# Split operands of all matmuls at one place modulo 256 bytes, stationary weights 64 bytes behind it

## The chip, the cores and the metric

The kernel runs on one core of one Trainium2 chip. The metric is the device time of one execution in microseconds (us), the median of several runs. A core has TensorE (matmuls), VectorE (DVE), ScalarE (ACT), GpSimd (POOL) and SyncE (SP, which here issues most DMAs), a memory SBUF of 128 partitions for operands and a memory PSUM in which matmuls accumulate.

## The reference

Two blocks over 256 tokens of width 2048, batch 1, all in float32. Cut to what matters:

```python
for i in range(2):                                  # first block
    shift, scale, gate = split((silu(c) @ ada_w[i] + ada_b[i])[:, None, :], 3)
    h = rmsnorm(x, norm_g[i]) * (1.0 + scale) + shift
    y = retention_branch(h, ...) if i == 0 else mla_branch(h, ...)
    x = x + gate * y
x = rmsnorm(x, final_norm_g)
# second block
h = rms_norm(x, attn_norm_gain)                     # then h @ w_in, two kinds of attention,
x = x + mixed(h) @ w_out                            # outputs normed and concatenated
x = x + peer(rms_norm(x, ffn_norm_gain), ...)       # 16384 experts, 8 heads of top 16
out = rms_norm(x, final_norm_gain)
```

retention_branch projects h to q, k, v and g (12,288 columns), mla_branch to two latents, a rope key and g (3,136 columns). peer picks experts by two top-16 lists, and adds, for each token, gate * gelu(expert_down[e] . x) * expert_up[e] over its 128 experts.

## The kernel before

Activations stay in SBUF: x by tokens, and the normed h transposed (hT), so that channels lie on partitions. Weights stream from HBM in pieces of 1 MB: a tile raw of 128 x 2048 float32, which SP loads (line 179, 1184 or 1272), three buffers. Every large product is made of three matmuls on operands split in two: h = the value rounded to float32r, l = the rest. split() (lines 172 and 173) makes them, ACT the rounded half (wh), VectorE the rest (wl), in half tiles of 1,024 columns from a ring of four pairs (halves(), lines 164 to 169), and a fifth pair xh, xl while the experts' second product runs.

Which operand is stationary (loaded as weights of TensorE, 128 columns of it) and which moves differs by place in the program:

- proj_steps (lines 243 to 245): the activations are stationary (hT, zT, zT1, ckvT, cqT, mT, and in the last part of the retention two wide tiles named v and sg), the streamed weights move, mostly 512 columns at once; 424, 416, 384, 272 and 256 in some blocks. For each k of a half tile it does two token blocks of three matmuls.
- turned_steps (lines 271 to 273) for q and k of the retention: the streamed weights are stationary, hT moves, 256 columns.
- hidden() (lines 1214 to 1216), the first product of peer, for all 128 blocks of 128 experts: the expert weights are stationary, hT moves, 256 columns.
- up_steps (lines 1294 to 1296), the second product of peer: the gated hidden values are stationary (Wh, Wl of pool up), the expert weights move (wh, wl or xh, xl), 512 columns.

SBUF is given out in pools, one behind the other: keep, stream (raw, wh, wl), small (tiny tiles), and behind them the pools of a phase (ret, mla, mlah, mix, peer, up and their w). A tile takes its bytes for each partition, rounded up to 32; the first tile of keep lies at byte 16,512, which is 128 modulo 256. Working through the sizes in order gives where operands start modulo 256 bytes. Tiles whose size is no multiple of 256 (colv 928 bytes, cst 4,896, mhalf 32, cact 64, A1 and B1 64 each) stand among the large ones in keep, so that hT starts at 32 and stream at 224. All slices of the operands are multiples of 256 bytes apart, but for the halves of weight pieces with 424, 416 and 272 columns.

| Operand | modulo 256 |
|---|---|
| hT (keep); cqT, ckvT (mla); zT1 (mlah) | 32 |
| raw, wh, wl (stream) | 224 |
| zT and the wide tiles v, sg (ret) | 96 |
| mT (mix) | 64 |
| Wh, Wl, xh, xl (up) | 224 |

The order of work is the program's: background generators (self.bg, tick()) put attention, norms and gates between the steps of projections at fixed rates. ACT's and VectorE's instructions run in the order written, and so do the DMAs that stand in ACT's own queue (nc.scalar.dma_start). cst holds identity, ones, a triangle, an iota, the causal and the dilated masks and small tables, loaded once (line 409). latent() is the second layer, mixed() the attention of the second block; at the start of mixed(), renorm() loads four pieces of a gain on ACT's queue (line 957), which line 967 multiplies in.

Of the kernel before, what the change touches and what calls it, by code (L numbers as in the profile page):

```python
# [10 lines left out]
F32 = mybir.dt.float32  # L11
# [113 lines left out]
class Net:  # L125
    def __init__(self, ctx, tc, a):
        self.ctx, self.tc, self.nc, self.a = ctx, tc, tc.nc, a
        self.keep = ctx.enter_context(tc.tile_pool(name="keep", bufs=1))
        self.st = ctx.enter_context(tc.tile_pool(name="stream", bufs=1))
        self.sm = ctx.enter_context(tc.tile_pool(name="small", bufs=1))  # L130
        self.dr = ctx.enter_context(tc.tile_pool(name="dram", bufs=1, space=bass.MemoryType.DRAM))
        self.ps = ctx.enter_context(tc.tile_pool(name="psum", bufs=1, space=PSUM))
        self.bg = []
        self.nhalf, self.extra = 0, None
        self.places = places()
# [251 lines left out]
    def start(self):  # L387
        nc, keep, a = self.nc, self.keep, self.a
        self.ident = keep.tile([128, 128], F32, name="ident")
        self.colv = keep.tile([128, V_END], F32, name="colv")  # L390
        nc.scalar.dma_start(self.colv, a["vectors"])
        nc.sync.dma_start(self.ident, a["consts"][:, C_ID:C_ID + 128])
        self.cst = keep.tile([128, C_END], F32, name="cst")
        self.xf = [keep.tile([128, D], F32, name=f"x{tb}") for tb in range(2)]
        for tb in range(2):
            nc.scalar.dma_start(self.xf[tb], a["x"][0, tb * 128:tb * 128 + 128, :])
        self.xt = [[self.xf[tb][:, cb * 512:cb * 512 + 512] for cb in range(4)] for tb in range(2)]
        self.mhalf = keep.tile([128, 8], F32, name="mhalf")
        nc.vector.memset(self.mhalf, -0.5)

        self.cact = keep.tile([128, 16], F32, name="cact")
        th = self.tiny(16)
        cc = self.colv[:, V_C:V_C + 16]
        nc.scalar.activation(th, cc, AF.Tanh, scale=0.5)
        nc.vector.scalar_tensor_tensor(th, th, 1.0, cc, op0=OP.add, op1=OP.mult)
        nc.vector.tensor_scalar(self.cact, th, 0.5, None, op0=OP.mult)
        self.ones = self.cst[:, C_ONE:C_ONE + 128]
        self.onesr = keep.tile([128, 128], F32R, name="onesr")
        nc.scalar.dma_start(self.cst, a["consts"])

        nc.vector.tensor_scalar(self.colv[:, V_GN:V_GN + 32], self.colv[:, V_GN:V_GN + 32], 0.5, None, op0=OP.mult)

    def angles(self, pool):
# [5 lines left out]
        self.cos = keep.tile([128, 2, 32], F32, name="cos")  # L419
        self.sin = keep.tile([128, 2, 32], F32, name="sin")  # L420
# [8 lines left out]
        pi = keep.tile([128, 2], I32, name="posi")  # L429
        nc.scalar.dma_start(pi, pos.rearrange("o (b p) -> p (o b)", p=128))  # L430
        pf = keep.tile([128, 2], F32, name="posf")
# [146 lines left out]
    def retention(self):  # L578
# [3 lines left out]
        self.A1 = keep.tile([128, 16], F32, name="A1")  # L582
        self.B1 = keep.tile([128, 16], F32, name="B1")
        with self.phase("ret", 8), self.tc.tile_pool(name="ret", bufs=1) as pool:
            A = pool.tile([128, 16], F32, name="A0")
            B = pool.tile([128, 16], F32, name="B0")
# [195 lines left out]
    def latent(self):  # L782
        nc, a = self.nc, self.a
        w_in, w_out, w_uq, w_ukv = "mla_w_in", "mla_w_out", "mla_w_uq", "mla_w_ukv"
        causal = self.cst[:, C_CAUSAL:C_CAUSAL + 256]
        scale = float(192 ** -0.5)
        with self.phase("mla", 7), ExitStack() as es:
            pool = es.enter_context(self.tc.tile_pool(name="mla", bufs=1))
            G = pool.tile([128, D], F32, name="G1")
            front = ExitStack()  # L790
# [4 lines left out]
            ss = pool.tile([128, 4], F32, name="latss")  # L795
# [16 lines left out]
            def latents():  # L812

                lr = pool.tile([128, 4], F32, name="latr")
# [126 lines left out]
            fa = self.keep.tile([128, 16], F32, name="fa")  # L941
# [6 lines left out]
            self.rtok = self.keep.tile([128, 2], F32, name="rtok")  # L948
# [25 lines left out]
    def mixed(self):  # L974
        nc, a = self.nc, self.a
        w_in, w_out = "w_in_2", "w_out_2"
        causal = self.cst[:, C_CAUSAL:C_CAUSAL + 256]
        with self.phase("mix", 8), self.tc.tile_pool(name="mix", bufs=1) as pool:
            hT, rtok = self.hT, self.rtok
            next(self.norms)  # L980
            norms = self.later(self.norms, 0.9)
            trig = pool.tile([128, 2, 2, 8], F32, name="trig")
            fb = pool.tile([128, 16], F32, name="fb")
            nc.sync.dma_start(fb, bass.AP(tensor=a["forget_bias_2"].tensor, offset=a["forget_bias_2"].offset,
                                          ap=[[0, 128], [1, 16]]))
            lf = pool.tile([128, 2, 16], F32, name="lf")
# [20 lines left out]
            cum = pool.tile([128, 2, 16], F32, name="cum")  # L1007
# [12 lines left out]
            def project(n, g, beside=iter(())):  # L1020
# [17 lines left out]
                for off in (0, 1024):  # L1038
                    def ev(tb, p, off=off):
# [5 lines left out]
                        dst = pool.tile([128, 1, 8, 66], F32, name="qk2", bufs=2)  # L1045
# [26 lines left out]
            def head(n, g, h):  # L1072
# [3 lines left out]
                else:  # L1076
                    mask = lambda tb: self.cst[:, C_DIL:C_DIL + 128] if tb == 0 else \
                        self.cst[:, C_DIL + 128:C_DIL + 384]
# [14 lines left out]
            def finish(n):  # L1093
# [7 lines left out]
                r = pool.tile([128, 2], F32, name=f"r_{n}")  # L1101
# [38 lines left out]
            self.rtok = self.keep.tile([128, 2], F32, name="rtok2")  # L1140
# [3 lines left out]
    def peer(self):  # L1144
# [5 lines left out]
        with self.phase("peer", 4), self.tc.tile_pool(name="peer", bufs=1) as pool:  # L1150
# [30 lines left out]
            def fetch(e):  # L1181
# [4 lines left out]
                for half in range(2):  # L1186
                    dh, dl = self.halves()
# [437 lines left out]
```

## Time and profile before

| | us |
|---|---|
| median of 3 runs | 3252.47 (3251.17 to 3254.47) |
| the profiled execution | 3252.83 |
| its span, first to last instruction | 3251.0 |
| TensorE busy with matmuls | 3159.2 (97%) |
| TensorE weight loads | 2762.0 (85%) |
| VectorE busy | 2366.0 (73%) |
| ScalarE busy | 1558.4 (48%) |
| moved from and to HBM | 216 GB/s over the span |

Matmuls follow each other in a pipeline: each is recorded from its start to its modelled end, and the next begins before that end. So a busy share of 97% doesn't say how fast TensorE works; the time from one start to the next does. Each matmul has its own weight load, which runs beside the matmul before it.

### The profile page before, as it was taken

The page shows a single profiled execution, that of the slowest core. Times are in us where ns is not written, and L with a number is a line of the kernel's source. Part 1 is how long each engine was busy: PE and PEld are TensorE (multiplying, and loading weights), DVE is VectorE, ACT ScalarE, POOL GpSimd, SP SyncE. Part 2 cuts the span into 40 slices and gives each one's busy share as a digit, 9 for nine tenths or more (in the row PEclk, how much of TensorE's full clock was granted, in tenths as well). Part 3 has the DMA queues.
Part 4 walks back from the last instruction along what each step waited for, and adds up shares of the span by engine and source line. Part 5 has one row for each costly group of instructions (what it writes and reads, how often), then busy time and mean ns, then how long its engine had stood idle before and what let it go on. Part 6 is the DMA issues. An engine that isn't in the chain of part 4 may idle for free.

```text
span 3251.0 us, 47605 instructions
## 1 busy us (share of the span) xinstructions
PE 3159.2 (97%) x18562; PEld 2762.0 (85%) x18562; DVE 2366.0 (73%) x3918; ACT 1558.4 (48%) x2162; POOL 414.4 (13%) x487
## 2 busy tenths in 40 slices
PE   4999999999999999999999999999999999999998
PEld 4888977887798888888888999999888898999987
DVE  6898878878787675455669966998766656556665
ACT  3444434344545455555554444555444444444444
POOL 0001210201000320000000312886000000000000
PEclk9999999999999999999999999999999999999999
DMA  8875677786585435444454456777966755555554
GB/s 342 305 268 203 244 270 296 254 300 243 202 289 201 143 130 196 144 153 145 143 185 152 158 198 212 260 242 258 314 238 235 239 201 207 196 202 186 194 194 142
DMA packets 141681, 705.68 MB, mean 217 GB/s; under 512 B 12680, under 2 KB 45832, under 8 KB 67728
## 3 DMA queue, kind: packets, MB, share of 16 engines
q1 hardware_dynamic: 139152, 696.51, 60.9%
q10 hardware_dynamic: 2304, 6.14, 0.5%
q8 instruction: 145, 2.38, 0.3%
q14 instruction: 80, 0.66, 0.1%
HBM read 676.38 MB, written 26.21 MB: 216 GB/s over the span
## 4 chain that ended last, share of the span: by engine, by line
PE 83%; DVE 8%; DMA 4%; issue 3%; ACT 1%; POOL 0%; SPq 0%; DVEq 0%; POOLq 0%; ACTq 0%
PE acc L244 11%; PE acc L245 11%; PE acc L243 11%; PE acc L1294 7%; PE acc L1296 7%; PE acc L1295 7%; PE tmp L1214 5%; PE tmp L1216 5%; PE tmp L1215 5%; DVE wl L173 3%; PE acc L272 2%; PE acc L273 2%; PE acc L271 2%; PE tmp L359 1%; PE acc L1214 1%
## 5 line engine op out<-in xcount | busy, mean ns | idle before, releaser
L173 DVE TENSOR_TENSOR wl<-raw,wh 128x1024 fp32r<-128x1024 f32 (+4 forms) x983 | 1197.2, 1225 | 469.9 <-ACT wh L172 467.6
L172 ACT ACTIVATE wh<-raw 128x1024 fp32r<-128x1024 f32 (+4 forms) x983 | 1018.3, 1044 | 1017.9 <-PE acc L245 343.6
L244 PE MATMUL acc<-wl,hTh 128*128 128x512 f32 (+4 forms) x1280 | 497.4, 389 | 13.1 <-DVE wl L173 13.1
L243 PE MATMUL acc<-wh,hTh 128*128 128x512 f32 (+4 forms) x1280 | 498.3, 391 | 1.5 <-ACT wh L172 1.5
L245 PE MATMUL acc<-wh,hTl 128*128 128x512 f32 (+4 forms) x1280 | 496.7, 388 | 0.0
L1214 PE MATMUL tmp<-hTh,wh 128*128 128x256 f32 x1280 | 361.5, 282 | 0.0
L1216 PE MATMUL tmp<-hTl,wh 128*128 128x256 f32 x1280 | 357.6, 279 | 0.0
L1215 PE MATMUL tmp<-hTh,wl 128*128 128x256 f32 x1280 | 357.5, 279 | 0.0
L1294 PE MATMUL acc<-wh,Wh 128*128 128x512 f32 x812 | 317.4, 391 | 2.8 <-ACT Wh L172 1.5
L1296 PE MATMUL acc<-wh,Wl 128*128 128x512 f32 x812 | 316.5, 390 | 0.9 <-DVE Wl L173 0.9
L1295 PE MATMUL acc<-wl,Wh 128*128 128x512 f32 x812 | 316.3, 390 | 0.0
L244 PEld LDWEIGHTS acc<-wl,hTh 128*128 128x128 f32 x1280 | 241.8, 189 | 63.1 <-DVE wl L173 18.4
L245 PEld LDWEIGHTS acc<-wh,hTl 128*128 128x128 f32 x1280 | 241.8, 189 | 47.9 <-DVE hTl L310 0.4
L243 PEld LDWEIGHTS acc<-wh,hTh 128*128 128x128 f32 x1280 | 241.2, 189 | 46.5 <-ACT wh L172 1.7
L1214 PEld LDWEIGHTS tmp<-hTh,wh 128*128 128x128 f32 x1280 | 240.4, 188 | 0.7
L1216 PEld LDWEIGHTS tmp<-hTl,wh 128*128 128x128 f32 x1280 | 240.9, 188 | 0.1
L1215 PEld LDWEIGHTS tmp<-hTh,wl 128*128 128x128 f32 x1280 | 239.7, 187 | 0.8
L1512 POOL TENSOR_SCALAR oh<-iota,slot 128x128 f16<-128x128 f16 x256 | 208.6, 831 | 168.6 <-DVE iota L1503 87.0
L471 DVE SCALAR_TENSOR_TENSOR w<-raw,cact,w 128x512 f32<-128x512 f32 x240 | 186.9, 779 | 23.1 <-DMA raw<-in_ada_dram 18.5
L1215 PE MATMUL acc<-hTh,wl 128*128 128x256 f32 x640 | 179.9, 281 | 6.9 <-DVE wl L173 6.9
L162 POOL TENSOR_TENSOR tiny<-tiny,mhalf 128x1 f32<-128x1 f32 (+1 forms) x23 | 18.8, 819 | 1303.6 <-DVE tiny L161 1303.6
L1294 PEld LDWEIGHTS acc<-wh,Wh 128*128 128x128 f32 x812 | 152.4, 188 | 36.5 <-DVE x L1303 2.9
(370 smaller groups left out, 5919.8 us busy)
## 6 DMA issues: line engine op xcount, KB each, us to landing
raw<-in_down_dram SPq DMA_DIRECT2D x128, 1024.0 KB, 5.0
raw<-in_up_dram SPq DMA_DIRECT2D x128, 1024.0 KB, 5.0
raw<-in_ret_w_in_dram SPq DMA_DIRECT2D x96, 1024.0 KB, 6.0
raw<-in_ada_dram SPq DMA_DIRECT2D x64, 1024.0 KB, 4.9
raw<-in_w_in_dram SPq DMA_DIRECT2D x44, 1024.0 KB, 4.9
raw<-in_ret_w_out_dram SPq DMA_DIRECT2D x32, 1024.0 KB, 4.9
G<-in_ada_first_dram SPq DMA_DIRECT2D x32, 512.0 KB, 5.8
raw<-in_mla_w_out_dram SPq DMA_DIRECT2D x16, 1024.0 KB, 4.9
```

Of the source, the lines that this page charges most:

```text
L172: self.nc.scalar.activation(h, raw, AF.Copy)
L173: self.nc.vector.tensor_tensor(l, raw, h.bitcast(F32), op=OP.subtract)
L243: nc.tensor.matmul(o, sh, wh[:, j, :], start=(k == 0), stop=False)
L244: nc.tensor.matmul(o, sh, wl[:, j, :], start=False, stop=False)
L245: nc.tensor.matmul(o, sl, wh[:, j, :], start=False, stop=(k == nk - 1))
L1214: nc.tensor.matmul(o, dh[:, s], hh[:, k % 4, :], start=(k == 0), stop=False)
L1215: nc.tensor.matmul(o, dl[:, s], hh[:, k % 4, :], start=False, stop=False)
L1216: nc.tensor.matmul(o, dh[:, s], hl[:, k % 4, :], start=False, stop=(k == 15))
L1294: nc.tensor.matmul(y[tb][c], Wh[:, s], uh[:, u], start=first, stop=False)
L1295: nc.tensor.matmul(y[tb][c], Wh[:, s], ul[:, u], start=False, stop=False)
L1296: nc.tensor.matmul(y[tb][c], Wl[:, s], uh[:, u], start=False, stop=last)
L1512: nc.gpsimd.tensor_scalar(oh2[:, t, :], iota, k2, None, op0=OP.is_equal)
```

## The change

A pool named little is added behind small, with a pad of 56 columns (224 bytes) in front. All tiles whose size is no multiple of 256 bytes move there, out of keep, ret, mla and mix (colv, cst, mhalf, cact, cos, sin, posi, posf, A0, B0, A1, B1, latss, latr, fa, rtok, rtok2, trig, fb, lf, cum, r_f, r_d). cst is cut to its first 456 columns; the causal mask is loaded again in latent(), both masks in mixed(), each with a DMA of its own on ACT's queue into a tile of the phase. qk2 is rounded up to 576 columns. So keep, stream, small and little have sizes that are multiples of 256 bytes, and by the same working all operands of split products start at 128 modulo 256.

The half tiles of halves() grow by 64 columns (256 bytes). Where the weights are stationary (turned_steps through weights(still=True), and fetch() of hidden()), the 1,024 columns used start 16 columns (64 bytes) later in the tile, at 192 modulo 256.

The diff, cut to its core; what is left out moves the other small tiles to self.little in the same way, or takes a mask from the new tiles:

```diff
@@ -31,11 +31,13 @@
 GSCALE = 65536.0
 S1 = 4
 HB = 4
+PAD = 56
+SHIFT = 16
 ADA_RATE = 0.3
 
 
-C_ID, C_ONE, C_TRI, C_IOTA, C_CAUSAL, C_DIL, C_COS2, C_SIN2, C_INVF, C_COLF, C_END = (
-    0, 128, 256, 384, 512, 768, 1152, 1168, 1184, 1216, 1224)
+C_ONE, C_TRI, C_IOTA, C_COS2, C_SIN2, C_INVF, C_COLF, C_CAUSAL, C_DIL, C_ID, C_END = (
+    0, 128, 256, 384, 400, 416, 448, 456, 712, 1096, 1224)
...
@@ -128,6 +130,10 @@
         self.keep = ctx.enter_context(tc.tile_pool(name="keep", bufs=1))
         self.st = ctx.enter_context(tc.tile_pool(name="stream", bufs=1))
         self.sm = ctx.enter_context(tc.tile_pool(name="small", bufs=1))
+
+
+        self.little = ctx.enter_context(tc.tile_pool(name="little", bufs=1))
+        self.little.tile([128, PAD], F32, name="pad")
...
-    def halves(self):
+    def halves(self, still=False):
 
         self.nhalf += 1
         if self.extra is not None and self.nhalf % (HB + 1) == 0:
-            return tuple(self.extra.tile([128, 1024], F32R, name=n, bufs=1) for n in ("xh", "xl"))
-        return tuple(self.st.tile([128, 1024], F32R, name=n, bufs=HB) for n in ("wh", "wl"))
+            t = [self.extra.tile([128, 1088], F32R, name=n, bufs=1) for n in ("xh", "xl")]
+        else:
+            t = [self.st.tile([128, 1088], F32R, name=n, bufs=HB) for n in ("wh", "wl")]
+        o = SHIFT if still else 0
+        return tuple(x[:, o:o + 1024] for x in t)
...
-    def weights(self, name, k, c0):
+    def weights(self, name, k, c0, still=False):
...
-            wh, wl = self.halves()
+            wh, wl = self.halves(still)
...
-            for wh, wl in self.weights(name, k0, c0):
+            for wh, wl in self.weights(name, k0, c0, True):
...
-        self.colv = keep.tile([128, V_END], F32, name="colv")
+        self.colv = self.little.tile([128, V_END], F32, name="colv")
...
-        self.cst = keep.tile([128, C_END], F32, name="cst")
+        self.cst = self.little.tile([128, C_CAUSAL], F32, name="cst")
...
-        nc.scalar.dma_start(self.cst, a["consts"])
+        nc.scalar.dma_start(self.cst, a["consts"][:, :C_CAUSAL])
...
+            causal = pool.tile([128, 256], F32, name="causal")
+            nc.scalar.dma_start(causal, a["consts"][:, C_CAUSAL:C_CAUSAL + 256])
...
+            masks = pool.tile([128, 640], F32, name="masks")
+            nc.scalar.dma_start(masks, a["consts"][:, C_CAUSAL:C_CAUSAL + 640])
+            causal, dil = masks[:, 0:256], masks[:, 256:640]
...
-                        dst = pool.tile([128, 1, 8, 66], F32, name="qk2", bufs=2)
+                        dst = pool.tile([128, 576], F32, name="qk2", bufs=2)[:, :528].rearrange("p (o h d) -> p o h d", o=1, h=8)
...
-                    dh, dl = self.halves()
+                    dh, dl = self.halves(True)
```

## Rows read from the trace of the kernel before

**Rows 1.** The page, parts 1 and 4: busy time, and the chain by engine.
```profile
PE 3159.2 (97%) x18562; PEld 2762.0 (85%) x18562; DVE 2366.0 (73%) x3918; ACT 1558.4 (48%) x2162; POOL 414.4 (13%) x487
...
PE 83%; DVE 8%; DMA 4%; issue 3%; ACT 1%; POOL 0%; SPq 0%; DVEq 0%; POOLq 0%; ACTq 0%
```

**Rows 2.** Stretches: window, length, busy (count) of each engine, clock, DMA share, GB/s.
```profile
660.73:716.26 55.53, 55.53 (x239) 44.80 (x238) 43.49 (x51) 24.70 (x30) 0.00 (x0) 1.00 0.85 306
809.54:840.92 31.38, 31.38 (x136) 25.44 (x135) 20.50 (x26) 15.20 (x23) 0.00 (x0) 1.00 0.56 198
1618.41:1639.02 20.61, 20.61 (x89) 16.59 (x88) 11.75 (x15) 9.40 (x13) 0.00 (x0) 1.00 0.49 173
2291.54:2335.08 43.54, 43.54 (x193) 35.88 (x192) 36.93 (x46) 21.64 (x26) 0.00 (x0) 1.00 1.00 333
```

**Rows 3.** Stretches with 256 moving columns, columns as in rows 2.
```profile
1886.31:1965.81 79.50, 79.50 (x676) 79.50 (x676) 47.28 (x50) 40.11 (x48) 0.00 (x0) 1.00 0.59 206
1854.38:1862.31 7.93, 7.93 (x71) 7.93 (x71) 7.93 (x20) 3.28 (x5) 2.81 (x4) 1.00 0.64 221
1224.89:1232.19 7.30, 7.30 (x64) 7.30 (x63) 5.25 (x12) 6.21 (x16) 0.71 (x1) 1.00 0.79 252
```

**Rows 4.** Groups by form: count | busy us, mean ns of one | idle before.
```profile
L243 PE MATMUL acc<-wh,hTh 128*128 128x512 f32 x1056 | 423.6, 403 | 1.5 <-ACT wh L172 1.5
...
L1214 PE MATMUL tmp<-hTh,wh 128*128 128x256 f32 x1280 | 361.5, 282 | 0.0
...
L1294 PE MATMUL acc<-wh,Wh 128*128 128x512 f32 x812 | 317.4, 391 | 2.8 <-ACT Wh L172 1.5 <-DVE x L1303 1.3
...
L271 PE MATMUL acc<-hTh,wh 128*128 128x256 f32 x512 | 146.8, 288 | 0.1
```

**Rows 5.** Stretches near the start, columns as in rows 2.
```profile
48.00:160.00 112.00, 108.95 (x573) 92.28 (x573) 92.69 (x102) 52.38 (x67) 0.00 (x0) 1.00 0.85 321
160.00:275.00 115.00, 113.55 (x597) 96.08 (x598) 105.82 (x141) 51.66 (x59) 8.88 (x8) 1.00 0.71 251
```

**Rows 6.** Timeline of TensorE, 272 columns: start us, us, engine, line, instruction.
```profile
1240.85 0.29 PE L243 MATMUL acc<-wh,hTh 128*128 128x272 f32 x1
...
1241.62 0.29 PE L243 MATMUL acc<-wh,hTh 128*128 128x272 f32 x1
...
1242.37 0.29 PE L243 MATMUL acc<-wh,hTh 128*128 128x272 f32 x1
...
1243.11 0.29 PE L243 MATMUL acc<-wh,hTh 128*128 128x272 f32 x1
```

**Rows 7.** Timeline of TensorE, 424 columns.
```profile
905.59 0.36 PE L243 MATMUL acc<-wh,hTh 128*128 128x424 f32 x1
...
906.72 0.36 PE L243 MATMUL acc<-wh,hTh 128*128 128x424 f32 x1
...
907.90 0.36 PE L243 MATMUL acc<-wh,hTh 128*128 128x424 f32 x1
```

**Rows 8.** The page, part 5: the two instructions of a split.
```profile
L173 DVE TENSOR_TENSOR wl<-raw,wh 128x1024 fp32r<-128x1024 f32 (+4 forms) x983 | 1197.2, 1225 | 469.9 <-ACT wh L172 467.6
L172 ACT ACTIVATE wh<-raw 128x1024 fp32r<-128x1024 f32 (+4 forms) x983 | 1018.3, 1044 | 1017.9 <-PE acc L245 343.6
```

**Rows 9.** DMA issues: queue, operation, count, KB each.
```profile
cst<-in_consts_dram ACTq DMA_DIRECT2D x1, 612.0 KB
```

**Rows 10.** Timeline of ACT and of VectorE at the start of mixed().
```profile
1224.05 0.36 ACTq L957 DMA_DIRECT2D w<-in_final_norm_g_dram  x1
...
1230.42 2.74 DVE L967 SCALAR_TENSOR_TENSOR x<-x,tiny,w 128x512 f32<-128x512 f32 x4 [0.82 <-POOL tiny L162]
```

**Rows 11.** Timeline of TensorE, f16 matmuls of 128 columns.
```profile
2205.31 1.07 PE L1530 MATMUL acc<-oh,oh 128*128 128x128 f16 x16
2206.18 0.37 PE L1214 MATMUL tmp<-hTh,wh 128*128 128x256 f32 x1
```

More of the change, by code (lines that the diff above doesn't have):

```diff
@@ L397, in start @@
         self.xt = [[self.xf[tb][:, cb * 512:cb * 512 + 512] for cb in range(4)] for tb in range(2)]
-        self.mhalf = keep.tile([128, 8], F32, name="mhalf")
+        self.mhalf = self.little.tile([128, 8], F32, name="mhalf")
         nc.vector.memset(self.mhalf, -0.5)
-        self.cact = keep.tile([128, 16], F32, name="cact")
+        self.cact = self.little.tile([128, 16], F32, name="cact")
         th = self.tiny(16)
@@ L418, in angles @@
         self.sinT = pool.tile([128, 256], F32, name="sinT")
-        self.cos = keep.tile([128, 2, 32], F32, name="cos")
-        self.sin = keep.tile([128, 2, 32], F32, name="sin")
+        self.cos = self.little.tile([128, 2, 32], F32, name="cos")
+        self.sin = self.little.tile([128, 2, 32], F32, name="sin")
         pos = a["positions"]
@@ L428, in angles @@
         nc.vector.tensor_copy(self.onesr, self.ones)
-        pi = keep.tile([128, 2], I32, name="posi")
+        pi = self.little.tile([128, 2], I32, name="posi")
         nc.scalar.dma_start(pi, pos.rearrange("o (b p) -> p (o b)", p=128))
-        pf = keep.tile([128, 2], F32, name="posf")
+        pf = self.little.tile([128, 2], F32, name="posf")
         nc.vector.tensor_copy(pf, pi)
@@ L581, in retention @@
         keep = self.keep
-        self.A1 = keep.tile([128, 16], F32, name="A1")
-        self.B1 = keep.tile([128, 16], F32, name="B1")
+        self.A1 = self.little.tile([128, 16], F32, name="A1")
+        self.B1 = self.little.tile([128, 16], F32, name="B1")
         with self.phase("ret", 8), self.tc.tile_pool(name="ret", bufs=1) as pool:
-            A = pool.tile([128, 16], F32, name="A0")
-            B = pool.tile([128, 16], F32, name="B0")
+            A = self.little.tile([128, 16], F32, name="A0")
+            B = self.little.tile([128, 16], F32, name="B0")
             G = pool.tile([128, D], F32, name="G0")
@@ L784, in latent @@
         w_in, w_out, w_uq, w_ukv = "mla_w_in", "mla_w_out", "mla_w_uq", "mla_w_ukv"
-        causal = self.cst[:, C_CAUSAL:C_CAUSAL + 256]
         scale = float(192 ** -0.5)
@@ L794, in latent @@
             lat = {}
-            ss = pool.tile([128, 4], F32, name="latss")
+            ss = self.little.tile([128, 4], F32, name="latss")
             for n, c0 in (("q", 0), ("kv", 512)):
@@ L812, in latents @@
             def latents():
-                lr = pool.tile([128, 4], F32, name="latr")
+                lr = self.little.tile([128, 4], F32, name="latr")
                 self.rsqrt(lr, ss, 1.0 / 512, 4)
@@ L938, in latent @@
             self.done(beside)
-            fa = self.keep.tile([128, 16], F32, name="fa")
+            fa = self.little.tile([128, 16], F32, name="fa")
             nc.vector.tensor_tensor(fa, self.colv[:, V_FN:V_FN + 16], self.colv[:, V_AT:V_AT + 16], op=OP.mult)
@@ L947, in latent @@
             next(cols)
-            self.rtok = self.keep.tile([128, 2], F32, name="rtok")
+            self.rtok = self.little.tile([128, 2], F32, name="rtok")
             self.norms = self.renorm(ss)
@@ L1006, in ev_forget @@
                 nc.vector.scalar_tensor_tensor(lf[:, tb, :], f, 0.0, ln, op0=OP.min, op1=OP.subtract)
-            cum = pool.tile([128, 2, 16], F32, name="cum")
+            cum = self.little.tile([128, 2, 16], F32, name="cum")
             def forget():
@@ L1076, in head @@
                 else:
-                    mask = lambda tb: self.cst[:, C_DIL:C_DIL + 128] if tb == 0 else \
-                        self.cst[:, C_DIL + 128:C_DIL + 384]
+                    mask = lambda tb: dil[:, 0:128] if tb == 0 else dil[:, 128:384]
                 def done(o, rd):
@@ L1100, in finish @@
                 nc.vector.tensor_reduce(s2, ss.rearrange("p (b c) -> p b c", b=2), axis=AX.X, op=OP.add)
-                r = pool.tile([128, 2], F32, name=f"r_{n}")
+                r = self.little.tile([128, 2], F32, name=f"r_{n}")
                 self.rsqrt(r, s2, 1.0 / 1024, 2)
@@ L1139, in mixed @@
             self.squares(ss, 3)
-            self.rtok = self.keep.tile([128, 2], F32, name="rtok2")
+            self.rtok = self.little.tile([128, 2], F32, name="rtok2")
             nc.vector.tensor_copy(self.rtok, self.rstd(ss))
```

7 lines of the change are left out of this document (3 added, 4 removed).

## The prediction

> **What bounds the kernel now.** First the page's first and fourth parts [rows 1]: TensorE has matmuls in flight 97% of the span, and the chain that ended last is TensorE for 83%, VectorE for 8%, DMA for 4%. So time falls if matmuls follow each other faster, and nearly nothing else matters. The mean length of one matmul says nothing of that, since neighbours overlap in the pipeline. What counts is the step from one start to the next. I read it from long runs in which TensorE waits for nothing: length of the stretch, divided by the matmuls that began in it (in the rows with their counts, one less than the count, since one had begun before; two less in the row at 1224.89).
>
> With 512 moving columns [rows 2]: 55.53 / 238 = 233.3 ns, 31.38 / 135 = 232.4, 20.61 / 88 = 234.2, and 43.54 / 192 = 226.8. With 256 columns [rows 3]: 79.50 / 675 = 117.8 ns, 7.93 / 70 = 113.3, 7.30 / 62 = 117.7. The other engines don't make these differences: the row with 226.8 ns has the highest DMA share (1.00) and VectorE busy for 85% of it, the row with 234.2 ns has 0.49 and 57%. [...] What differs is where the operands lie. I call an address modulo 256 bytes its place, and the difference the place of the stationary operand less that of the moving one. In the order of rows 2: moving weights at 224 and stationary hT at 32 (difference 64); ret's tiles at 96 (128); mT at 64 (96); and Wh with uh, both at 224 (0). Equal places are the fastest by 5.6 to 7.4 ns. In rows 3 the first two have hT moving at 32 and weights stationary at 224 (difference 192), the third is a difference of 64.
>
> **The change, part by part.** Shifts between operands. By the declared sizes every split operand goes to place 128, and the stationary weights of turned_steps and hidden() to 192.
>
> *(a) proj_steps, 512 columns: difference 64, 128 or 96 becomes 0.* Each of the lines 243 to 245 has 1,056 such matmuls with hT [rows 4] and, by the loops, 576 with the other stationary tiles: zT, mT, zT1, ckvT and the two halves of a wide tile. By difference, over three lines: 3 x 1,248 at 64, 3 x 256 at 128, 3 x 128 at 96. At the step of the row with equal places: 3,744 x 6.5 + 768 x 5.6 + 384 x 7.4 ns = 24.3 + 4.3 + 2.8 = 31.4 us. The 192 with 384 columns, scaled by 0.75: 0.9 us. Sum 32.3 us. Of that 712 x 6.5 = 4.6 us lie between 48 and 275 us, where DMA is busy 0.85 and 0.71 of the time at 321 and 251 GB/s and VectorE up to 92% [rows 5]; I let half of it count. Of the other 27.7 I take 0.93, for waits for wl and raw that get longer when TensorE asks sooner. Together 2.3 + 25.7 = 28 us. Bounds: 0, if equal places aren't the reason, and the whole 32.3.
>
> *(b) turned_steps and hidden(), 256 columns: difference 192 becomes 64.* 2,048 matmuls on each of lines 1214 to 1216 (128 experts of 16) and 512 on each of 271 to 273 [rows 4], 7,680 in all, so each ns is 7.7 us. No row of before has this pair with hT moving. The nearest have the same difference with the roles exchanged: at 256 columns 117.7 ns, no gain; at 272 columns, in blocks of six matmuls, (1241.62 - 1240.85) / 6 = 128 ns at difference 0, 125 at 192, and 123 at 64 [rows 6], where 0.01 us of resolution is 1.7 ns. So the gain from 192 to 64 lies between 0 and 1.7 ns; I take 0.4, near the row of the same length: 7,680 x 0.4 = 3 us less. The bounds are far apart. Below: the run of 113.3 ns [rows 3] at the unchanged places, which began after a wait and kept its rhythm to the next wait, shows that 4.5 ns less is possible: 35 us. Above: 128 ns against 125 for difference 0 at 272 columns says that another place can cost 3 ns, 23 us.
>
> *(c) up_steps: 224 and 224 become 128 and 128.* Same difference, so 0; 1,024 matmuls on each of three lines by the loops, 812 of them with wh [rows 4], so 3.1 us for each ns if the place itself matters and not the difference alone. For that there is one pair of rows: with 424 columns the weights of j = 0 lie at 224 and those of j = 1 at 128, against the same hT, and six matmuls take 906.72 - 905.59 = 1.13 us at 224 and 907.90 - 906.72 = 1.18 us at 128 [rows 7], so 188 against 197 ns. Its difference changes too (64 to 160), so it doesn't tell which it is; it sets the rival below. These 424 and 416 columns keep mixed differences after the change; I give them 0.
>
> *(d) splits and small tiles.* ACT and VectorE do the same instructions. A half tile costs ACT 1.04 us (L172) and VectorE 1.23 us (L173) [rows 8], beside 2.8 us of matmuls (24 x 117.8 ns), or 2.7 at 113.3; they stay hidden. Without that cover each half tile would wait for both, 2.3 us. Small tiles, pads and the larger halves move addresses only: 0.
>
> *(e) loads.* The first load of cst (612 KB [rows 9]) shrinks by 3,072 of 4,896 bytes a partition, 0.39 MB; at the 321 GB/s of rows 5 that is 1.2 us, in a start that DMA sets: 1 us less. Two loads come on ACT's queue: causal in latent() and masks in mixed(). A wait there would hold the weight splits queued behind it. Neither adds one that I can see: ACT's instructions ahead of each need the last output() to be over already, and that is what frees the memory. masks (0.33 MB) stands ahead of the four loads of fg; the first fg is issued at 1224.05 and its user runs at 1230.42 on the chain [rows 10], so with 1.0 us more in front (0.33 MB at the same rate): 1 us later. Together 0.
>
> **Sum.** -28 - 3 - 1 + 1 = -31 us. The profiled execution took 3252.83 us, 0.4 over the median, so 3252.83 - 31 = 3221.8: I say 3222, its own range 3208 to 3235.
>
> [...]
>
> **Rivals.**
> 1. *256 columns fall into the fast rhythm.* If difference 64 lets hidden() and turned_steps keep the step of 113.3 ns, then 35 x 0.95 = 33 us instead of 3: 3192. For it: the rhythm exists, at the same lengths. Against: 62 matmuls at difference 64 stayed at 117.7. Chance 0.22.
> 2. [...] Sixteen f16 matmuls of 128 columns start at 54 ns each (0.87 us from 2205.31 to 2206.18 [rows 11]); at that rate 512 columns take 218 and 256 take 109. Then (a), 4,896 matmuls, gains 4,896 x 9 = 44 us more, (c) 3,072 x 9 = 28, (b) 7,680 x 8.8 = 68 instead of 3: about 3252.8 - 0.95 x 172 = 3089. No fp32r row comes near. Chance 0.04.
> 3. *No change: it isn't the place.* proj_steps and up_steps differ otherwise too (which operand is reused, how long a group of accumulations is); if that makes the 6.5 ns, all stays: 3252. Against: three stationary tiles in the same proj_steps already give 232.4, 233.3 and 234.2. The same time results if the shift doesn't reach the operands. Chance 0.14.
> 4. *Slower: the moving operand's own place decides, and 128 is a bad one.* 197 / 424 columns is 0.464 ns a column, 233.3 / 512 is 0.456, 226.8 / 512 is 0.443. At 0.464 a matmul of 512 columns takes 237.6: (a) +4.3 x 4,896 = 21 us, (c) +10.8 x 3,072 = 33; (b) at 118.8 +1.0 x 7,680 = 8. That is 3252.8 + 62 = 3315; with only half of it 3284. It decides as soon as up_steps, where no difference changes, steps above 229 ns. Chance 0.12.
>
> **How the numbers follow.** The forecast has 0.48, the rivals 0.22, 0.04, 0.14 and 0.12. About 0.2% (6.5 us) is what a measurement of this kernel can tell from no change. Faster: 0.48 + 0.22 + 0.04 = 0.74; same 0.14; slower 0.12. The range leaves out rivals 2 and 4 (0.16) and takes in 1 and 3: 3182 to 3257.
>
> **What would show it.** In the profile after: stall-free runs of lines 243 to 245 at 227 ns (a), of 271 to 273 and 1214 to 1216 at 117 (113 for rival 1), of 1294 to 1296 still at 226.8 (c; above 229 for rival 4). The prediction is wrong if 243 to 245 stay at 233, or if 1294 moves by more than 2 ns either way.

## The result, and the profile after

The changed kernel takes 3225.12 us (median of 4 runs, 3222.64 to 3229.81), the kernel before 3252.53 beside it (3251.17 to 3254.47): 0.992 of it, 95% interval 0.9905 to 0.9936. The forecast was 3222, so the time and its main cause came out. Two terms of the sum had other sizes, one of them for another reason than was given, and the two errors nearly cancel.

The line numbers of the new file are 9 higher at proj_steps (252 to 254), turned_steps (280 to 282) and split() (181, 182), and 11 higher at hidden() (1225 to 1227), up_steps (1305 to 1307) and the f16 matmuls (1541).

The page of after, part 1, answers to the first of [rows 1]:

```profile
PE 3128.8 (97%) x18562; PEld 2757.6 (86%) x18562; DVE 2365.1 (73%) x3918; ACT 1557.0 (48%) x2162; POOL 420.0 (13%) x487
```

The same instructions, the same 97%; VectorE's and ACT's busy time moved by 1 us. TensorE did the same work in 30 us less. Where, the stretches show (window, length, busy and count of each engine, granted clock, DMA share, GB/s; steps are one less than TensorE's count, or two less where two matmuls had begun before). With 512 columns: proj_steps with hT, with zT (at 96 before, like the v and sg of the row at 809.54), with mT, and up_steps, for the four of [rows 2]:

```profile
650.88:704.15 53.27, 53.27 (x236) 44.08 (x235) 41.99 (x48) 23.21 (x29) 0.00 (x0) 1.00 0.85 314
441.84:466.08 24.24, 24.24 (x108) 20.09 (x107) 21.69 (x24) 6.47 (x7) 6.27 (x4) 1.00 0.73 259
1628.82:1639.48 10.66, 10.66 (x49) 8.77 (x47) 6.77 (x10) 5.95 (x12) 0.00 (x0) 1.00 0.45 153
2307.48:2350.77 43.29, 43.29 (x192) 35.70 (x191) 31.38 (x37) 20.85 (x25) 0.00 (x0) 1.00 0.84 285
```

53.27 / 235 = 226.7 ns a step (233.3 before), 24.24 / 107 = 226.5 (232.4), 10.66 / 47 = 226.8 (234.2), 43.29 / 191 = 226.6 (226.8); the granted clock is 1.00 in these four rows as in [rows 2]. Now hidden(), for [rows 3]:

```profile
1752.81:1787.92 35.11, 35.11 (x312) 35.11 (x311) 34.22 (x124) 14.75 (x19) 5.82 (x5) 1.00 0.43 151
1861.39:1940.88 79.49, 79.49 (x676) 79.49 (x676) 47.29 (x50) 40.07 (x48) 0.00 (x0) 1.00 0.59 206
2601.47:2612.77 11.30, 11.30 (x97) 11.30 (x96) 5.60 (x5) 4.74 (x5) 0.00 (x0) 1.00 0.53 187
```

35.11 / 310 = 113.3 ns, but 79.49 / 675 = 117.8 and 11.30 / 96 = 117.7 at the same difference of 64 bytes. So there isn't one step for this difference; there are two, and each of these runs kept one of them throughout.

To set whole kernels side by side I took the step from start to start of every float32r matmul of a profiled execution. As a yardstick I use a line through 109.1 ns at 256 columns and 215.7 at 512; I chose it, no run shows it as a step, and it only sorts the steps. A step over 1.3 times the yardstick counts as a wait, and what it takes above the yardstick as waiting time; the others make the mean. Columns: mean step in ns of proj_steps with 512 columns (some 4,600 steps), of turned_steps (1,500), hidden() (6,070) and up_steps (3,056); all waiting time and the medians in us. The kernels e1 to e5 are those of the experiments below.

| kernel | proj_steps | turned | hidden | up | waiting | median |
|---|---|---|---|---|---|---|
| before | 233.3 | 117.4 | 117.7 | 227.2 | 98.3 | 3252.5 |
| after | 227.9 | 115.8 | 117.0 | 227.1 | 100.2 | 3225.1 |
| e1_proj64 | 233.4 | 115.2 | 116.5 | 227.1 | 96.9 | 3242.2 |
| e2_still192 | 227.9 | 117.5 | 117.3 | 227.0 | 102.8 | 3229.5 |
| e3_still0 | 227.9 | 119.9 | 119.9 | 227.1 | 97.9 | 3247.4 |
| e4_place0 | 227.9 | 115.8 | 117.0 | 227.1 | 99.5 | 3221.2 |
| e5_still224 | 227.9 | 116.9 | 116.9 | 227.1 | 104.1 | 3226.7 |

From before to after, steps times counts: -24.9 us in proj_steps with 512 columns, -2.5 in turned_steps, -4.5 in hidden(), -0.2 in up_steps, waits +1.9, and the rest of the float32r steps (424, 416, 384, 272 and 256 columns in proj_steps) -0.5; together -30.7, where the spans differ by 3251.0 - 3220.9 = 30.1.

### The profile page after: what moved, and what is told of

It is laid out like the page before. It is cut to its first block, busy times and chain, and to the rows that moved or that the text cites. A ratio compares the mean times of both kernels' runs of the same rounds, so it can differ in the third digit from the quotient of the medians.

```text
span 3220.9 us, 47602 instructions
## 1 busy us (share of the span) xinstructions
PE 3128.8 (97%) x18562; PEld 2757.6 (86%) x18562; DVE 2365.1 (73%) x3918; ACT 1557.0 (48%) x2162; POOL 420.0 (13%) x487
## 4 chain that ended last, share of the span: by engine, by line
PE 63%; DVE 6%; DMA 1%; issue 1%; POOL 1%; ACT 1%; POOLq 0%; DVEq 0%; SPq 0%; ACTq 0%
PE acc L1305 7%; PE acc L1307 7%; PE acc L1306 7%; PE acc L252 6%; PE acc L254 6%; PE acc L253 6%; PE tmp L1225 5%; PE tmp L1227 5%; PE tmp L1226 5%; DVE wl L182 2%; PE tmp L368 1%; PE acc L1226 1%; PE acc L1227 1%; PE acc L1225 1%; PE acc L1541 1%
```

## Experiments

**One part at a time.** The theory: the step hangs on the difference of the operands' places modulo 256, and not on the places themselves or on how the loops are built. e1 shifts only the moving weights of proj_steps back to the old difference:

```diff
-        o = SHIFT if still else 0
+        o = 48 if still == "proj" else SHIFT if still else 0
-            for wh, wl in self.weights(name, k0 + kg, c0):
+            for wh, wl in self.weights(name, k0 + kg, c0, "proj"):
```

> The changed kernel, but the streamed weights that move in proj_steps start 48 columns (192 bytes) later, at place 64; the stationary activations stay at 128, so the difference is 64 again, as it was for hT before. All else is as in the changed kernel. Theory (the difference sets the step): stall-free runs of proj_steps with 512 columns go back from 227 to 233 ns, and the time rises by 4,896 x 5.4 ns x 0.95 = 25 us over the changed kernel, to about 3249. Rival (the moving operand's own place, or anything else that the change moved): the step stays near 227 and the time at 3225.

It took 3242.19 us (0.9973 of before, 0.9964 to 0.9983), 17 us over after. The stretch of proj_steps with hT:

```profile
656.61:712.37 55.76, 55.76 (x240) 44.92 (x239) 44.29 (x52) 25.47 (x30) 0.00 (x0) 1.00 0.82 309
```

55.76 / 239 = 233.3 ns, to a tenth what it was before, with nothing changed but 192 bytes of address. So the rival that the loops make the 6.5 ns is out. The time is 7 us less than the theory had: proj_steps alone is 25.5 us slower than in after (81.4 against 55.9 us above the yardstick), but hidden() and turned_steps came out 4 us faster than in after, at unchanged addresses, and 3 us of waits went. That the same 64 bytes gave 116.5 here and 117.0 there is no effect of e1's edit that these runs show: two executions of after differ as much in hidden() ("Side by side" below), though no other execution had the 115.2 of turned_steps.

e2 and e3 set the stationary weights' difference to what it was, and to none:

```diff
-SHIFT = 16
+SHIFT = 48        # e2: difference 192;  e3: SHIFT = 0
```

> The changed kernel with SHIFT = 48 columns: the stationary weights of turned_steps and hidden() lie at place 64, a difference of 192 to hT, as before the change. Theory: those 7,680 matmuls go back from means of 117.0 and 115.8 ns to 117.7 and 117.4, with hardly any of them in the rhythm of 113; the time rises by 7 us, to about 3232. Rival (the rhythm after a wait is chance, and the difference of 64 does nothing): no change, 3225.

> The changed kernel with SHIFT = 0: the stationary weights of turned_steps and hidden() lie at place 128 like hT, difference 0. Theory: equal places are the best for 512 columns and the worst for 256, where the 96 matmuls of 256 columns in mixed() step 119.5 ns at difference 0; then 7,680 x 2.6 ns = 20 us more, to about 3245. Rival (equal places are best for all lengths): a step of 114 or less and 3205.

e2: 3229.48 us (0.9928, 0.9914 to 0.9942), 4 over after; e3: 3247.43 (0.9982, 0.9973 to 0.9991), 22 over after. Both as the theory had them within 3 us. The interval of e2 overlaps that of after, so for the difference of 192 the steps tell and not the time, and they bear the theory out in part only: 6% of turned_steps were under 115.5 ns (46% in after), but 30% of hidden() ahead of the gates still were. The long run of hidden(), 79.49 us in after, in e3:

```profile
1870.55:1951.40 80.85, 80.85 (x676) 80.85 (x675) 47.46 (x50) 39.98 (x48) 0.00 (x0) 1.00 0.58 202
```

80.85 / 674 = 120.0 ns. What is best with 512 columns, no difference, is the slowest of the four differences that the kernels here had with 256: 7,600 steps at a mean of 119.9 instead of 117.0 and 115.8. Had the stationary weights not been set 64 bytes behind, the change would have brought some 4 us instead of 27 (e3 against the 3251.68 of the kernel before beside it).

e4 adds 128 unused bytes in front of keep, so that all operands stand at place 0 (stationary weights at 64):

```diff
+        keep.tile([128, 32], F32, name="shiftall")
```

> The changed kernel with 128 unused bytes in front of keep: every operand starts at place 0 instead of 128 (192 becomes 64), all differences are unchanged. Theory: steps and time stay as they are, 3225 within 5 us. Rival (the operand's own place counts): up_steps and proj_steps leave 227 ns, and each ns is 8 us.

3221.15 us (0.9906, 0.9891 to 0.9921), and its row of the table is that of after but for the waits. At the differences of this kernel the place itself does nothing; that was the rival on the slow side. No profile here prints an address, so the places are worked out from the sizes; that they are right is borne out by e1, e3 and e5, whose steps are those that the maps below give for their differences.

**A map of differences.** map1 is a kernel of bare matmuls: groups of 48 for each difference in steps of 16 bytes, the moving operand at 128 or 160, behind a wait or behind four f32 matmuls.

> No part of the reference is computed: x is copied to the output, and TensorE runs 128 groups of 48 fp32r matmuls in threes (h with h, h with l, l with h), 256 or 512 moving columns, moving operand at place 128 or 160, stationary operand 0 to 240 bytes behind it in steps of 16, each group once right after a wait and once right after four float32 matmuls of 128 columns. It measures the step by itself. Theory (the difference sets the step): the groups at places 128 and 160 agree within 1 ns at each difference; at 512 columns difference 0 gives 227 ns, 64 gives 233; at 256 columns 0 gives 119 to 120, 64 and 192 give 113 or 118 depending on how the group began. Rival (the moving operand's own place): the two places differ by 2 ns or more at equal differences.

Mean of the last 24 steps of a group, in ns; two numbers where the four groups of a difference don't agree:

| difference | 512 columns | 256 columns | | difference | 512 columns | 256 columns |
|---|---|---|---|---|---|---|
| 0 | 226.7 | 120.0 | | 128 | 232.1, 233.3 | 118.8, 120.0 |
| 16 | 233.3 | 118.3 | | 144 | 233.3 | 116.7 to 120.0 |
| 32 | 233.3 | 118.3 | | 160 | 233.3 | 120.0 |
| 48 | 233.3 | 117.8, 123.3 | | 176 | 230.0 | 118.1 |
| 64 | 233.3 | 113.3, 117.8 | | 192 | 228.9 | 117.8 |
| 80 | 232.1 | 118.7 | | 208 | 232.0, 233.3 | 116.7 |
| 96 | 234.4 | 117.4, 118.6 | | 224 | 233.3 | 116.7 |
| 112 | 233.3 | 120.0 | | 240 | 226.7, 228.3 | 117.5, 120.0 |

(The first group of all, 256 columns at no difference, is left out: it began with steps of 213 ns, which no other group had, and ended at 120.) With 512 columns the two places agree within 1.6 ns at every difference. With 256 they don't at all of them, so there the theory's test failed: at 240 bytes both groups at 128 gave 120.0 and both at 160 gave 117.5, at 144 it was 120.0 twice against 116.7 and 118.3, and the 123.3 at 48 and the 113.3 at 64 came in one group of four each, at 160 behind f32 matmuls. Whether the place or the start makes these, the map can't tell. Stretches of it, 512 columns, at 0 and at 64, and 256 columns at 64, once after a wait and once behind f32 matmuls:

```profile
835.24:845.69 10.45, 10.45 (x48) 8.63 (x46) 0.00 (x0) 0.00 (x0) 0.00 (x0) 1.00 0.01 2
932.63:943.36 10.73, 10.73 (x47) 8.65 (x46) 0.00 (x0) 0.00 (x0) 0.00 (x0) 1.00 0.00 0
278.07:283.60 5.53, 5.53 (x48) 5.53 (x48) 0.00 (x0) 0.35 (x1) 0.00 (x0) 1.00 0.01 3
284.62:289.84 5.22, 5.22 (x49) 5.22 (x47) 0.00 (x0) 0.00 (x0) 0.00 (x0) 1.00 0.00 0
```

These are 46, 46, 47 and 46 steps, the first ones of a group included: 10.45 / 46 = 227.2 and 10.73 / 46 = 233.3 with VectorE idle and DMA at most at 0.01, so no other engine makes the difference. The last two are the same matmuls at the same places: 5.53 / 47 = 117.7 and 5.22 / 46 = 113.5. What they were preceded by is all that differs. It doesn't decide alone: the group behind f32 matmuls with the moving operand at 128 stayed at 117.8.

**Another good difference, and what sets the rhythm.** In all four groups of the map 208 and 224 bytes give 116.7 ns.

```diff
-SHIFT = 16
+SHIFT = 56        # difference 224
```

> The changed kernel with the stationary weights at a difference of 224 bytes in place of 64. Theory (the difference of places sets the step, and a map made of bare matmuls holds in the kernel): 116.7 ns a step in all runs of 256 columns, none at 113.3; against the changed kernel's means of 117.0 ns (6070 steps of hidden) and 115.8 ns (1496 steps of turned_steps) that is -1.8 us and +1.3 us: 3224.6 us, with hidden and turned_steps at one step. Rival (what a run starts with sets the step, and places only shift the odds): runs at 113.3 ns stay in some fifth of the steps, 3222 to 3227 us. Rival (the map does not carry over, since in the kernel other engines write SBUF beside the matmuls): 117.8 ns or more everywhere, +4.9 and +3.0 us, 3233 us.

3226.67 us (0.9919, 0.9906 to 0.9932). The stretch of hidden():

```profile
1867.62:1946.47 78.85, 78.85 (x677) 78.85 (x677) 47.34 (x50) 40.21 (x48) 0.00 (x0) 1.00 0.60 208
```

78.85 / 676 = 116.6 ns, and 116.9 over all of both stages, since some runs had 117.8, which the theory had excluded. With that, the map of bare matmuls holds in the kernel. As a choice 224 is no better than 64: what it gains in hidden() it loses in turned_steps, where 64 had more of the fast rhythm.

map2 puts one more matmul of 32 to 512 columns behind the 24th of a group of 72 with 256 columns. (Its places 0 and 32 are offsets in the tile, the 128 and 160 of map1.)

> No part of the kernel is computed: x is copied to the output, and 136 groups of 72 float32r matmuls of 256 columns (a stationary operand of 128 columns, used as in the kernel: high by high, high by low, low by high) run, the difference of places 64, 192, 208 or 224 bytes, the moving operand at place 0 or 32; behind the 24th matmul of a group one more of 32, 64, .. 512 columns is put in (none in one group of each kind). The map of differences before showed two lasting steps at 64 bytes, 117.8 and 113.3 ns, and one at the others (117.8 at 192, 116.7 at 208 and 224). Theory: the rhythm is not a matter of place but of how the matmuls stand in time when a run starts, so the matmul put in moves a group at 64 bytes from one step to the other for some of its lengths, at least 3 in 16; at the other differences the step is the same before and behind it. Rival: the rhythm is chosen once at the start of a group by the wait ahead of it; the matmul put in changes nothing, and behind it the step is what it was before it, in all 16. Second rival: 113.3 ns is there at any difference if the start is right; then some of the 48 matmuls behind run at 113.3 ns at 192, 208 or 224 too.

At 64 bytes all 30 groups that had one inside (the one of 32 columns ran elsewhere) ran at 113.3 ns ahead of it; behind it 10 kept 113.3 and 20 ran at 117.8, by its length (192, 224, 256, 288 and 384 columns kept it, with both places of the moving operand alike). At 192 bytes 8 of 30 had 113.3 ahead of it, and 6 of these 8 had 117.8 behind it. At 208 all had 116.7, and at 224 116.7 or 117.8, some changing at the matmul put in. So one step whatever happens, which the theory had for the other three differences, is there at 208 only. The timeline of TensorE where 64 columns went in at 64 bytes (start us, us, engine, line, instruction):

```profile
36.09 0.28 PE L45 MATMUL acc<-mov,sta 128*128 128x256 f32 x1
36.20 0.28 PE L46 MATMUL acc<-mov,sta 128*128 128x256 f32 x1
36.32 0.19 PE L43 MATMUL tmp<-mov,sta 128*128 128x64 f32 x1
36.34 0.36 PE L44 MATMUL acc<-mov,sta 128*128 128x256 f32 x1
36.55 0.28 PE L45 MATMUL acc<-mov,sta 128*128 128x256 f32 x1
36.66 0.28 PE L46 MATMUL acc<-mov,sta 128*128 128x256 f32 x1
36.78 0.28 PE L44 MATMUL acc<-mov,sta 128*128 128x256 f32 x1
36.90 0.28 PE L45 MATMUL acc<-mov,sta 128*128 128x256 f32 x1
```

The 64 columns start 0.02 us ahead of the next matmul, and that one holds 0.21 us: together two steps. From there on the rhythm is the slow one, with nothing else changed. So the place doesn't set it, and a rhythm, once there, lasted to the end of the group. That it is a matter of how the matmuls stand to each other in time fits this, but is argued and not shown. The second rival, 113.3 at any difference, holds for 64 and 192 only.

**The seams of the kernel.** After up_steps each pair of experts in hidden() ran at 117.8 ns in both kernels. map3 repeats that seam (24 steps of 512 columns at no difference, then 72 of 256) with six ways across it, and the seam with 16 f16 matmuls.

> No part of the kernel is computed: x is copied to the output, and 128 groups of float32r matmuls repeat the two seams of the kernel's last 1200 us. 96 groups: 24 steps of 512 columns at a difference of 0 (as up_steps), then 72 steps of 256 columns (stationary operands high, low, high, as hidden) at a difference of 0, 16, .. 240 bytes, with six ways across the seam: plain; a matmul of 384 columns more; one of 64 columns more; the order high by high, high by low, low by high; the first matmul in two halves of 128 columns; the last of 512 in two halves of 256. 32 groups: 16 float16 matmuls of 128 columns, then 60 steps of 256, plain and in the other order. Theory (the step is set by the difference and, at 64 bytes, by what the run comes from): the plain way at 64 bytes gives 117.8 ns, as after 512 columns in the changed kernel, and at least one of the five other ways gives 113.3 ns; at 208 bytes every way gives 116.7, at 0 every way 120. Rival (a run's rhythm hangs on things outside TensorE, such as other engines' writes to SBUF): the plain way at 64 bytes gives 113.3 ns in these groups, in which no other engine works beside TensorE. Second rival (the seam decides nothing, only the difference and the order of the operands): all ways with the same order have the same step at 64 bytes.

At 64 bytes, the last 48 steps: plain 117.8, 384 columns more 113.3, 64 columns more 113.3, the other order of operands 117.8, the first matmul in two halves 113.3, the last of 512 in two halves 117.8; behind f16 matmuls 113.3 plain and 117.8 in the other order. At 208 every way gave 116.7 and at 0 every way 120.0, as at these differences in the first map. Plain and with 64 columns more:

```profile
83.55:89.20 5.65, 5.65 (x50) 5.65 (x49) 0.00 (x0) 0.00 (x0) 0.00 (x0) 1.00 0.01 3
567.56:573.00 5.44, 5.44 (x51) 5.44 (x49) 0.00 (x0) 0.00 (x0) 0.00 (x0) 1.00 0.01 3
```

48 steps each: 5.65 / 48 = 117.7 and 5.44 / 48 = 113.3.
The plain seam reproduces the kernel's 117.8 with no other engine at work, so it doesn't take their writes. The f16 seam doesn't reproduce it (113.3 here, 117.8 in the kernel); what differs there I don't know.

**Into the kernel.** e6 adds the 64 columns where a pair of experts starts behind up_steps; the result is overwritten by the next matmul:

```diff
+                    if k == 0 and e >= N0 and e % 2 == 0:
+                        nc.tensor.matmul(o[:, :64], dh[:, s], hh[:, 0, :64], start=True, stop=True)
                     nc.tensor.matmul(o, dh[:, s], hh[:, k % 4, :], start=(k == 0), stop=False)
```

> The changed kernel with one matmul of 64 columns more (its result is overwritten by the next) at the start of each pair of experts in hidden behind up_steps, 22 in all. In the map of seams 72 steps of 256 columns behind 512 columns took 9.041 us at 117.8 ns plain and 8.847 us with the 64 columns more, at 113.3 ns. Theory (the rhythm at 64 bytes hangs on what a run comes from): the 22 runs of 96 steps go from 117.8 to 113.3 ns, each 0.194 + 24 x 0.0045 = 0.302 us shorter: 6.6 us, 3218.5 us from the changed kernel's 3225.1. Rival (in the kernel the other engines' writes set the rhythm): the runs stay at 117.8 ns and the matmul costs 22 x 0.114 us = 2.5 us more: 3227.6 us. Second rival (the steps get shorter and the time does not, since the weights' loads set this stage): runs at 113.3 ns, 3225 us, with the gain turned into waits ahead of up_steps.

e7 also makes two halves of the first matmul behind each set of f16 matmuls (kick is set there):

```diff
+                    if k > 0 and kick:
+                        for u in (slice(0, 128), slice(128, 256)):
+                            nc.tensor.matmul(o[:, u], dh[:, s], hh[:, k % 4, u], start=False, stop=False)
```

> As the kernel with 22 matmuls of 64 columns more, and beside it the first matmul behind each of the 32 sets of 16 float16 matmuls in two halves of 128 columns. In the changed kernel the 59 steps behind such a set all ran at 117.8 ns. Theory: half a matmul moves them to 113.3 ns, 59 x 4.45 = 263 ns less at some 143 ns for the split (9.041 - 8.860 = 0.181 us gained in 72 steps of the map, of 0.324): 0.12 us for each of 30 runs, 3.6 us: 3214.9 us. Rival (behind float16 matmuls the rhythm is set otherwise, as plain runs behind them had 113.3 ns in the map and 117.8 here): they stay at 117.8 ns and the split costs 32 x 0.11 us = 3.7 us: 3222.2 us.

e6: 3218.62 us (0.9904, 0.9887 to 0.992). e7: 3218.01 (0.9894, 0.9877 to 0.991). The first run of 96 that was shown of after, in e6, and a run behind f16 matmuls in after and in e7:

```profile
2603.47:2614.23 10.76, 10.76 (x96) 10.76 (x96) 5.59 (x5) 4.52 (x5) 0.00 (x0) 1.00 0.55 196
```

```profile
2010.86:2017.81 6.95, 6.95 (x60) 6.91 (x60) 6.95 (x19) 2.79 (x4) 6.11 (x8) 1.00 0.75 216
```

```profile
2007.16:2013.73 6.57, 6.57 (x59) 6.54 (x58) 6.57 (x19) 4.13 (x6) 5.91 (x8) 1.00 0.87 227
```

10.76 / 95 = 113.3 ns for 117.7; 6.95 / 59 = 117.8; 6.57 / 58 = 113.3. The whole stage from the first to the last matmul of up_steps, hidden() in between, takes 942.3 us in e6 (2263.53 to 3205.82) and 948.6 in after (2261.59 to 3210.16): 6.3 us, for 6.6 expected. In e7 the gates' stage is 4.2 us shorter too (240.2 us from its first to its last f16 matmul, 244.5 in after), but the median is that of e6 within its interval, 3 us over the theory. Where those 4 us went in the profiled execution, the next part shows.

**Side by side.** After and e6 again, on one chip:

> The changed kernel again, on the same chip as the next one, so that the two can be set side by side. Every theory: 3225 us within 4 us. If the two rhythms at 64 bytes fall by chance in turned_steps and in the part of hidden ahead of the gates, some 3500 steps at 113.3 or 117.8 ns, then its times differ by several us between executions, at most 16 us.

> The kernel with 22 matmuls of 64 columns more again, beside the changed kernel. Theory: 6.6 us below it, 3218.5 us within 4 us, and the 22 runs behind up_steps at 113.3 ns in this execution as in the one before. Rival (the gain seen before was the chance of a fast rhythm in the earlier stages, 113.6 ns against 115.3 there): within 2 us of the changed kernel.

3223.17 us (3219.88 to 3226.21; 0.9911, 0.9897 to 0.9924) and 3219.07 (3216.59 to 3223.89; 0.9898, 0.9883 to 0.9913): 4 us less, between the theory's 6.6 and the rival's 2; the intervals overlap. With the runs of the first time, 9 of after have a median of 3224.1 and 8 of the kernel with 64 columns more 3218.6. Its stage of up_steps took 943.5 us (2267.96 to 3211.43), 951.5 in the other (2260.07 to 3211.58). So the kernel with the 64 columns is faster than after by 4 to 5.5 us in the medians, and its stage of up_steps by 6 to 8.

The executions also show one thing that differs between runs of one kernel, whose times spread over some 10 us. Mean step of the 1,985 matmuls of hidden() ahead of the gates in four profiled executions: after 115.3 (57% under 115.5 ns) and 113.7 (93%), e6's kernel 113.6 (95%) and 115.3 (58%). The instructions and addresses are the same; the share in the fast rhythm isn't. But the second execution of after, with the faster hidden(), was not faster (span 3222.3 against 3220.9). The chain at the end of the gates, in the first and in the second:

```profile
2250.09 9.97 DMA gt<-gates
...
2260.18 1.29 DVE W L1275 x2
...
2263.27 0.50 PE acc L1307
2263.77 0.23 PE acc L1305
```

```profile
2246.16 12.38 DMA gt<-gates
2258.66 1.29 DVE W L1275 x2
...
2261.75 0.80 PE acc L1307
2262.54 0.43 PE acc L1305
```

The last f16 matmul came 3.7 us earlier (2234.49 against 2238.20), the load of the gates ended only 1.5 us earlier (2258.54 against 2260.06), and the first matmul of up_steps started 2.97 us after the last of hidden() instead of 0.79 (timeline of TensorE, first and second; idle time in brackets):

```profile
2261.59 0.50 PE L1305 MATMUL acc<-wh,Wh 128*128 128x512 f32 x1 [0.51 <-ACT Wh L181]
```

```profile
2260.07 0.50 PE L1305 MATMUL acc<-wh,Wh 128*128 128x512 f32 x1 [2.69 <-ACT Wh L181]
```

Behind that wait up_steps ran with a step of 0.43 us up to 2268.09, where the first execution had 0.23. The granted clock in the same seven us, first and second:

```profile
2263.00:2270.00 7.00, 6.73 (x30) 5.55 (x30) 6.86 (x10) 3.55 (x7) 0.00 (x0) 1.00 0.97 375
```

```profile
2263.00:2270.00 7.00, 7.00 (x21) 5.46 (x21) 7.00 (x9) 2.93 (x4) 0.00 (x0) 0.65 0.81 312
```

The granted clock was 1.00 after the short wait and 0.65 on average after the long one: nine matmuls fewer. Of the 3.7 us gained up to the last f16 matmul, 2.2 went into the time from there to up_steps, which the load of the gates ends, and the stage of up_steps took 2.9 more (951.5 against 948.6). In e7 likewise: the start of up_steps came 2.29 us after the matmul before it, the granted clock was 0.52 in the same seven us, and the stage took 946.4 us against 942.3 in e6. The row of e7, and rows of seven early us of up_steps in e6 and in the second execution of its kernel, e9:

```profile
2263.00:2270.00 7.00, 6.32 (x14) 4.50 (x15) 7.00 (x10) 4.26 (x7) 0.00 (x0) 0.52 0.85 321
```

```profile
2265.00:2272.00 7.00, 6.79 (x30) 5.63 (x31) 7.00 (x10) 4.16 (x7) 0.00 (x0) 1.00 0.87 329
```

```profile
2270.00:2277.00 7.00, 7.00 (x25) 5.61 (x24) 7.00 (x10) 3.23 (x5) 0.00 (x0) 0.76 0.88 324
```

So a fast hidden() doesn't bring the lower clock by itself: e6 had the fast one, started up_steps 1.68 us after the matmul before it and kept 1.00; e9 had the slow one, started it after 2.46 us and had 0.76.

## Why the prediction was right, point by point

- *(a) proj_steps.* Right in place and cause, the size a little off. The steady step went to 226.7 as [rows 2] had it for equal places, and e1, e4 and map1 show that the difference alone does it. The gain was 24.9 us in steps, where the sum had 32.3 in all and 28 after allowances. The mis-sized term is the 6.5 ns per matmul: on average it was 233.3 - 227.9 = 5.4, since the first steps behind a wait, or behind other matmuls, are now longer than the steady ones, and I took the steady step for all. Over the whole trace of after the first six steps take 230.8 ns, the next six 227.9 and all later ones 226.7; in the kernel before it is 233 from the first on. One such start in after:

```profile
708.23 0.39 PE L253 MATMUL acc<-wl,hTh 128*128 128x512 f32 x1
...
709.62 0.39 PE L253 MATMUL acc<-wl,hTh 128*128 128x512 f32 x1
...
710.99 0.39 PE L253 MATMUL acc<-wl,hTh 128*128 128x512 f32 x1
```

  Six steps in 1.39 us (232 ns), the next six in 1.37 (228). The allowance for waits and for the stretch between 48 and 275 us (4.3 us) was too much: all waiting grew by 1.9.
- *(b) turned_steps and hidden().* -7.0 us for -3, inside its bounds but by another way. I read one step for the difference from rows of other shapes [rows 3, 6]; there are two, 117.8 and 113.3, and the change raised the share of the fast one, from 8% to 46% of turned_steps and from 7% to 57% of hidden() ahead of the gates, and left it at 0 or 1% behind f16 matmuls and behind up_steps (fast: under 115.5 ns). So rival 1 came true in part. The row against it, 62 matmuls at 64 bytes that stayed at 117.7, was one run of one start: it couldn't exclude what another start does. The bound above, that another place costs 3 ns, was real: 119.9 at no difference (e3).
- *The sum.* In steps (a) and (b) gave 24.9 + 7.0 = 31.9 us where the sum had 28 + 3 = 31: (a) brought 3 less and (b) 4 more. That the forecast came so close is in part luck. And 57% was one execution's share; in the second (e8) it was 93%, so (b) is no single size.
- *(c) up_steps.* 0, right: 227.2 and 227.1. Rival 4, with its test at 229 ns, falls with it and with e4. The 424 columns [rows 7] step 191.7 ns in after and in e4 alike, so there too the places alone do nothing.
- *(d), (e).* Splits: nothing, as said. Loads: the first matmul of turned_steps began at 47.51 us instead of 48.01, half a us less for 1, but with the same load it began at 46.19 in e8 and at 48.43 in e9, so no gain can be told from it; nor can the load of the masks be told from the other waits.
- *Rivals 2 and 3.* e1 against after shows that for float32r the addresses alone make the difference: 233.3 against 226.7 ns. Rival 3 falls with it. Rival 2, with 218 ns for 512 columns, had no row for it after either; 226.6 is the best with 512 columns.
- *Open.* Why the addresses matter no run here shows; the maps give the steps, not the cause. What starts the fast rhythm is known for some seams only.

## What to carry to other kernels

When one engine is busy all the time, compare its steps from start to start between stages that do the same instruction; a steady difference of 3% is worth looking for in the operands' addresses before the loops (here 233.3 against 226.7 ns, and in e1 the addresses alone made it). The best difference of places was another for each shape here (map1: 0 bytes gave 226.7 ns with 512 columns but 120.0 with 256, where 208 and 224 gave 116.7 and 64 gave 113.3 or 117.8), so map it with bare matmuls before moving a kernel's memory. A run that can fall into two rhythms (here 113.3 and 117.8 ns) has no single cost: look at how many of its runs are in each and what comes ahead of them, and ask what the time gained will wait for at the stage's end.

## What the hardware showed that I had not expected

- A step of back-to-back float32r matmuls that depends on the difference of the two operands' addresses modulo 256: 226.7 to 234.4 ns with 512 columns, 113.3 to 123.3 with 256 (map1). The addresses themselves made at most 1.6 ns with 512 columns (map1) and nothing in the kernel when all moved by 128 bytes (e4: 227.9 ns in proj_steps, as in after); with 256 columns the map leaves it open at 48, 64, 144 and 240 bytes.
- Two lasting steps, 113.3 and 117.8 ns, for the same instructions at 64 bytes, and the same at 192 (map2). At 64 bytes one matmul of 64 columns put into a fast run made the rest of it slow (map2); put ahead of a run behind 512-column matmuls it made the slow one fast (map3), and 22 of them shortened a stage by 6 us (e6).
- After 2.69 us without a matmul the granted clock was 0.65 on average from 2263 to 2270 us, and the step of up_steps 0.43 us up to 2268.09; after 0.51 us without one it was 1.00 in the same stretch, and the step 0.23 (e8 against after).
